# Spreading 1/rms over a tile: two products with ones and diagonals in place of eight narrow products

## The chip, the cores and the metric

The kernel runs on one core of a Trainium2 chip. A core has a matrix engine (TensorE, "PE" in the profile, its weight loads "PEld"), two elementwise engines that can read the matrix engine's accumulator PSUM (VectorE, "DVE", and ScalarE, "ACT"), a third one for data in SBUF alone (GpSimd, "POOL"), and SyncE ("SP"), which issues transfers. Each engine works through its own queue in order, and semaphores make one wait for another. The metric is the time of one execution on the device in microseconds; shown is the median of several runs.

## The reference

One decoder layer on x of 2048 rows by 1024 columns, float32:

```
hn   = rmsnorm(x, norm1_g)
proj = hn @ w_in                      # u_pool (512) | q | k | v (512 each)
mixed = concat(rmsnorm(pool_mixer(u_pool)), rmsnorm(stick_breaking(q, k, v)))
h = x + mixed @ w_out
h = h + square(relu(rmsnorm(h) @ w_up)) @ w_down
y = rmsnorm(h)
# rmsnorm(x, g) = x * rsqrt(mean(x*x, over columns) + 1e-6) * g
```

What matters here is rmsnorm: each row of the sequence has one factor 1/rms, and every value of that row is multiplied by it.

## The kernel before

Activations are held transposed: a tile has 128 features in its partitions and 512 rows of the sequence along its free dimension, so the 2048 rows make four row blocks (`j` = 0 to 3) of eight feature chunks each. In this layout the factor 1/rms differs along the free dimension and is the same in all 128 partitions. To multiply by it with an elementwise engine, the 512 factors have to stand in every partition; bringing them there is the "spread".

Every matrix product is done in three passes of a split of both operands into a high and a low part (`split`, L143 and L144: ACT copies to the reduced type, DVE subtracts), which gives the three lines L172 to L174 of `products`.

A normalisation goes through these steps:

- `add_square` (L177): ACT squares a chunk into a buffer tagged `nt` (pool `ntp`, three buffers), and DVE adds it to the tile `ss`.
- `mean_squares` (L194): tiny products (eight instructions) with a column 1/n sum `ss` over the partitions, 128 rows of the sequence at a time, into four columns of PSUM (`pm`, L199).
- `inv_root` (L203): DVE takes the four columns out of PSUM (L207), and then POOL (in one early case DVE) computes the inverse root on a tile of 128x4: one integer operation and three Newton steps.
- in `inv_rms`, `yr` (L235, L236) becomes the high and the low part of these 128x4 factors: factor number 128*b + p stands in partition p, column b.
- `spread` (L221): for each of the four columns b and for high and low part, one product whose stationary operand is the column repeated 128 times and whose moving operand is the identity `identr`; eight products of 128 columns each write a tile `pr` of 128x512 in PSUM.
- ACT copies `pr` to SBUF as `r` (L245), and `normed` (L251) multiplies each chunk by its gain and by `r` (L257, tile `nt`) and splits the result into `h` or `mix`. For the first row block the products are made with x before it is normalised, and `r` is applied when they leave PSUM (L373, L418, L430).

`inv_rms` is used in the front of the kernel: for the first norm of the four row blocks, for the pooled part and for the attention part of each, and for the second norm of row blocks 0 and 1. The second norm of blocks 2 and 3 (`root_last`, with spreads inside `up`) and the final norm (`final_root`, `final_put`) call `spread` directly.

The front runs input projections, the pool mixer and the attention together: `prog` is a list of projection steps, `run` (L1256) emits them one after the other, and between them takes pieces of normalisation from the list `later` and pieces of attention from `todo`. A scheduling pass then orders each engine's queue by priority and by the times that it expects instructions to be ready. The body of `inv_rms` has high priority. `gates` makes TensorE's steps after a certain count stand behind the sums (`pm`) and behind the spread (`pr`). After the front, from about 700 us on, come the two large products `up` (L983) and `down` (L1218). A second version of the whole attention stands in a branch at the end that these inputs don't take.

Of the kernel before, what the change touches and what calls it, by code (L numbers as in the profile page):

```python
# [8 lines left out]
F32 = mybir.dt.float32  # L9
F32R = mybir.dt.float32r  # L10
BF16 = mybir.dt.bfloat16
I32 = mybir.dt.int32
AF = mybir.ActivationFunctionType
ALU = mybir.AluOpType

P = 128
# [11 lines left out]
TB = T // P  # L28
# [18 lines left out]
def hymba_block(ctx: ExitStack, tc: tile.TileContext, xT, gains, w_in, pool_w, w_out, w_up, w_down, out):  # L47
    nc = tc.nc
# [3 lines left out]
    const = pool("const", 1)  # L52
# [43 lines left out]
    ident = const.tile([P, P], F32, name="ident")  # L96
    make_identity(nc, ident)
    identr = const.tile([P, P], F32R, name="identr")
    nc.vector.tensor_copy(identr, ident)
    identb = const.tile([P, P], BF16, name="identb")  # L100
    nc.vector.tensor_copy(identb, ident)
    maskb = const.tile([P, 2, P], BF16, name="maskb")
# [44 lines left out]
    marks, gates = {}, []  # L147
# [46 lines left out]
    def mean_squares(parts, n, where=None, tag="px"):  # L194

        pm = (where or psx).tile([P, T], F32, tag=tag, name="pm")
        for c in range(TB):
            for i, ss in enumerate(parts):
                marks["pm"] = nc.tensor.matmul(pm[:, c:c + 1], ss[:, c * P:(c + 1) * P], inv[n],  # L199
                                               start=(i == 0), stop=(i == len(parts) - 1))  # L200
        return pm[:, 0:TB]

    def inv_root(pm, eng):  # L203

        v, w = vp.tile([P, 3 * TB], F32, tag="v", name="v"), pm.shape[-1]
        m, y, t = v[:, 0:w], v[:, TB:TB + w], v[:, 2 * TB:2 * TB + w]
        nc.vector.tensor_scalar(m, pm, 1.0, EPS, op0=ALU.mult, op1=ALU.add)  # L207
        eng.tensor_scalar(y.bitcast(I32), m.bitcast(I32), -0.5, float(0x5F3759DF), op0=ALU.mult, op1=ALU.add)
        for _ in range(3):
            if eng is nc.vector:  # L210
                eng.scalar_tensor_tensor(t, y, -0.5, y, op0=ALU.mult, op1=ALU.mult)
                eng.tensor_tensor(t, t, m, ALU.mult)
                eng.scalar_tensor_tensor(y, t, 1.5, y, op0=ALU.add, op1=ALU.mult)
            else:
                eng.tensor_tensor(t, y, y, ALU.mult)
                eng.tensor_tensor(t, t, m, ALU.mult)
                eng.tensor_scalar(t, t, -0.5, 1.5, op0=ALU.mult, op1=ALU.add)
                eng.tensor_tensor(y, y, t, ALU.mult)
        return y

    def spread(pr, yr):  # L221

        for b in range(TB):
            for x in range(2):
                mm = nc.tensor.matmul(pr[:, b * P:(b + 1) * P], yr[:, x, b:b + 1].to_broadcast([P, P]), identr,  # L225
                                      start=(b == 0 and x == 0), stop=(b == TB - 1 and x == 1), skip_group_check=True)
        return mm

    def inv_rms(ss, n, r=None, eng=None, early=False):

        eng = eng or nc.gpsimd
        with tc.high_priority():
            y = inv_root(mean_squares([ss], n, psz if early else None, "pz" if early else "px"), eng)
            yr = tmp.tile([P, 2, TB], F32R, tag="yr", name="yr")
            eng.tensor_copy(yr[:, 0], y)  # L235
            eng.tensor_tensor(yr[:, 1], y, yr[:, 0].bitcast(F32), ALU.subtract)  # L236
            where, tag = (psx, "px") if eng is nc.vector else (psz, "pz") if early else (pst, "pt")
            pr = where.tile([P, T], F32, tag=tag, name="pr")
            marks["pr"] = spread(pr, yr)
            if eng is not nc.vector:  # L240
                g = state["tick"]
                gates.extend([(g + 10, marks["pm"]), (g + 14, marks["pr"])])
            if r is None:
                r = tmp.tile([P, T], F32, tag="r", name="r", bufs=2)
            nc.scalar.activation(r, pr, AF.Copy)  # L245
            return r

    def rms(chunks):
        return inv_rms(sum_squares(chunks), len(chunks) * P)
# [79 lines left out]
    def norm1_first():  # L329

        x, h = st[0]["x"], []
        for k in range(KD):
            d = make_h(0)
            a = nc.scalar.activation(d[:, 0], x[:, k], AF.Copy, scale=g1[:, k:k + 1])
            v = nc.vector.scalar_tensor_tensor(d[:, 1], x[:, k], g1[:, k:k + 1], d[:, 0].bitcast(F32),
                                               op0=ALU.mult, op1=ALU.subtract)
            h.append((d[:, 0], d[:, 1]))
        st[0]["h"] = h
        with tc.issue_after(a.ins), tc.issue_after(v.ins):
            ss = sum_squares([x[:, k] for k in range(KD)])  # L340
        st[0]["r"] = inv_rms(ss, D, root_tile(), nc.vector)

    def norm1_rms(j):
        def square(k):
            if k == 0:
                st[j]["ss"] = sum_tile()
            add_square(st[j]["ss"], st[j]["x"][:, k], k == 0)
        later.extend(lambda k=k: square(k) for k in range(KD))
        later.append(lambda: st[j].update(r=inv_rms(st[j]["ss"], D, root_tile() if j == 2 else None, early=j == 1)))
# [1046 lines left out]
```

## Time and profile before

| | |
|---|---|
| runs shown | 1949.64 us median of 3, 1944.7 to 1951.38 |
| profiled execution | 1947.63 us, its span 1945.8 us |
| granted TensorE clock, mean | 0.997 |
| busy PE / DVE / ACT / POOL | 1922.0 / 1267.6 / 954.2 / 201.2 us |

A row of the timeline reads: start and length in microseconds, engine, line, operation, written tile <- read tiles, shapes, count, and in square brackets how long the engine stood idle before it and for what. A row of the groups gives, after the bar, the busy time of the whole group in us and the mean length of one in ns, and after the next bar the idle time before them. A matmul's length in the timeline (0.39 us for 512 columns) is longer than the distance to the next one, since they are pipelined; the chain of work gives the distance.

### The profile page before, as it was taken

How to read it: one execution, taken by the hardware profiler on the slowest of the kernel's cores; microseconds unless marked ns; L12 is line 12 of the kernel's file. 1: busy time of each engine (PE TensorE's matmuls, PEld its weight loads, DVE VectorE, ACT ScalarE, POOL GpSimd, SP SyncE). 2: the span in 40 equal slices, each digit the busy share in tenths (PEclk: the TensorE clock that was granted, in tenths of full speed). 3: DMA queues.
4: the chain of work that ended last, by engine and by line, in shares of the span. 5: the costliest groups of instructions: out<-in, count | busy, mean ns of one | idle time of the engine just before them, and what ended most of it. 6: DMA issues, size and time to landing. Idle time of an engine off the chain costs nothing.

```text
span 1945.8 us, 26005 instructions
## 1 busy us (share of the span) xinstructions
PE 1922.0 (99%) x9139; PEld 1602.9 (82%) x9139; DVE 1267.6 (65%) x1882; ACT 954.2 (49%) x1544; POOL 201.2 (10%) x399
## 2 busy tenths in 40 slices
PE   9999999999999999999999999999999999999997
PEld 7888888888888888888878888878888888888887
DVE  6887799668866975777586565655554443446474
ACT  5565566455644555555575555553323232424353
POOL 0212113113211110000000000000110000213010
PEclk9999999999999999999999999999999999999999
DMA  6686686898796854677474534478876554646472
GB/s 216 205 263 200 205 287 200 259 323 281 247 386 219 322 200 149 217 242 252 171 244 155 173 141 163 148 253 292 299 273 196 194 195 152 199 156 205 150 253 89
DMA packets 164845, 426.79 MB, mean 219 GB/s; under 512 B 19680, under 2 KB 25824, under 8 KB 160608
## 3 DMA queue, kind: packets, MB, share of 16 engines
q1 hardware_dynamic: 164560, 424.77, 64.3%
q8 instruction: 74, 1.21, 0.3%
q14 instruction: 67, 0.55, 0.1%
q10 hardware_dynamic: 144, 0.26, 0.0%
HBM read 284.44 MB, written 140.51 MB: 218 GB/s over the span
## 4 chain that ended last, share of the span: by engine, by line
PE 93%; DVE 2%; DMA 2%; ACT 1%; issue 1%; POOL 1%; SPq 0%; ACTq 0%; DVEq 0%; POOLq 0%
PE pb L1218 31%; PE pY L983 17%; PE pZ L983 8%; PE pd L172 8%; PE pd L174 8%; PE pd L173 8%; PE pX L983 4%; PE po L676 2%; PE pta L669 1%; PE pr L225 1%; PE pz L611 1%; PE pz L612 1%; PE pm L199 1%; DMA wr<-in_w_down_dram 1%; PE pb L1181 1%
## 5 line engine op out<-in xcount | busy, mean ns | idle before, releaser
L1218 PE MATMUL pb<-ad,wd 128*128 128x512 f32 x2640 | 601.5, 390 | 1.6 <-ACT ad L143 1.0
L1218 PEld LDWEIGHTS pb<-ad,wd 128*128 128x128 f32 x2640 | 494.9, 188 | 104.8 <-ACT ad L143 1.6
L983 PE MATMUL pY<-sa,hw 128*128 128x512 f32 x1536 | 364.3, 389 | 2.2 <-ACT u L922 2.2
L983 PEld LDWEIGHTS pY<-sa,hw 128*128 128x128 f32 x1536 | 288.1, 188 | 62.7 <-ACT u L922 3.0
L172 PE MATMUL pd<-h,hl 128*128 128x512 f32 x752 | 299.0, 398 | 0.7 <-DVE qkr L418 0.7
L173 PE MATMUL pd<-h,hl 128*128 128x512 f32 x752 | 297.3, 395 | 0.0
L174 PE MATMUL pd<-h,hl 128*128 128x512 f32 x752 | 296.3, 394 | 0.9 <-DVE hl L144 0.9
L983 PE MATMUL pZ<-sa,hw 128*128 128x512 f32 x768 | 184.7, 389 | 1.4 <-DVE a L936 1.4
L143 ACT ACTIVATE ad<-ar 128x1024 fp32r<-128x1024 f32 x112 | 117.3, 1050 | 138.0 <-PE pb L1218 126.2
L144 DVE TENSOR_TENSOR wd<-wr,wd 128x1024 fp32r<-128x1024 f32 x64 | 82.8, 1294 | 151.0 <-ACT wd L143 150.8
L144 DVE TENSOR_TENSOR ad<-ar,ad 128x1024 fp32r<-128x1024 f32 x112 | 144.1, 1292 | 55.9 <-ACT ad L143 55.8
L143 ACT ACTIVATE wd<-wr 128x1024 fp32r<-128x1024 f32 x64 | 67.8, 1059 | 209.1 <-PE pb L1218 204.9
L983 PEld LDWEIGHTS pZ<-sa,hw 128*128 128x128 f32 x768 | 144.0, 188 | 31.6 <-DVE a L936 1.9
L174 PEld LDWEIGHTS pd<-h,hl 128*128 128x128 f32 x752 | 141.5, 188 | 29.2 <-DVE hl L144 1.4
L172 PEld LDWEIGHTS pd<-h,hl 128*128 128x128 f32 x752 | 141.8, 189 | 28.4 <-DVE qkr L418 1.0
L173 PEld LDWEIGHTS pd<-h,hl 128*128 128x128 f32 x752 | 141.5, 188 | 26.2
L143 ACT ACTIVATE hl<-raw 128x512 fp32r<-128x512 f32 x168 | 103.8, 630 | 106.5 <-PE pd L174 64.5
L144 DVE TENSOR_TENSOR hl<-raw,hl 128x512 fp32r<-128x512 f32 x168 | 114.0, 685 | 46.4 <-ACT hl L143 45.7
L144 DVE TENSOR_TENSOR hw<-rt,hw 128x512 fp32r<-128x512 f32 x128 | 87.5, 686 | 75.3 <-ACT hw L143 75.2
L983 PE MATMUL pX<-sa,hw 128*128 128x512 f32 x384 | 93.1, 389 | 0.0
L1013 DVE TENSOR_TENSOR wr<-wr 128x1024 f32<-128x1024 f32 x32 | 39.2, 1224 | 81.3 <-DMA wr<-in_w_down_dram 78.3
L922 ACT ACTIVATE u<-pY 128x512 f32<-128x512 f32 x64 | 38.1, 595 | 102.6 <-PE pY L983 102.4
(203 smaller groups left out, 2391.0 us busy)
## 6 DMA issues: line engine op xcount, KB each, us to landing
ar<-sd SPq DMA_DIRECT2D x112, 512.0 KB, 4.5
wr<-in_w_down_dram SPq DMA_DIRECT2D x72, 512.0 KB, 3.7
rb<-in_w_up_dram SPq DMA_DIRECT2D x32, 1024.0 KB, 5.9
sd<-a SPq DMA_DIRECT2D x128, 256.0 KB, 3.8
raw<-in_w_in_dram SPq DMA_DIRECT2D x50, 512.0 KB, 4.5
sd<-s SPq DMA_DIRECT2D x96, 256.0 KB, 3.7
raw<-in_w_out_dram SPq DMA_DIRECT2D x32, 512.0 KB, 4.9
sr<-su SPq DMA_DIRECT2D x28, 512.0 KB, 5.5
```

The lines of the kernel that those rows point to most:

```text
L143: nc.scalar.activation(hi, src, AF.Copy)
L144: return nc.vector.tensor_tensor(lo, src, hi.bitcast(F32), ALU.subtract)
L172: nc.tensor.matmul(ps, hl[:, 0, c], hi, start=(k == 0), stop=False)
L173: nc.tensor.matmul(ps, hl[:, 0, c], lo, start=False, stop=False)
L174: mm = nc.tensor.matmul(ps, hl[:, 1, c], hi, start=False, stop=(k == n - 1))
L199: marks["pm"] = nc.tensor.matmul(pm[:, c:c + 1], ss[:, c * P:(c + 1) * P], inv[n], start=(i == 0), stop=(i == len(parts) - 1))
L225: mm = nc.tensor.matmul(pr[:, b * P:(b + 1) * P], yr[:, x, b:b + 1].to_broadcast([P, P]), identr, start=(b == 0 and x == 0), stop=(b == TB ...
L676: nc.tensor.matmul(po[:, p * 256 + to:p * 256 + to + hi - lo], vw[:, 2 * p + v], at[:, x, lo:hi], start=(p == 0 and n == 0 and x == 0), sk ...
L922: nc.scalar.activation(k[name], y, AF.Copy)
L983: nc.tensor.matmul(t, w[:, wx, c], a[:, ax, c % 2], start=first and c == 0 and x == 0, stop=last and c == G - 1 and x == 2, skip_group_che ...
L1013: nc.vector.tensor_tensor(b, a, b, ALU.subtract)
L1218: nc.tensor.matmul(ps[q, n], t[:, wx, c, n * P:(n + 1) * P], left_[q][:, ax, c], start=(n_ in ("P1", "P5", "P2") and kk == 0 and c == 0 an ...
```

## The change

In `inv_rms` alone the call of `spread` is replaced. Two tiles of 128x4x128 (`diag`, taken from the `nt` buffers) get, in block b, the identity times column b of `yr`: DVE makes the one for the high part in a single product of two repeated operands, ACT the one for the low part in four copies of the identity with a scale per partition. Then two products of 512 columns, with a stationary 128x128 tile of ones (`onesr`, made once at the start by DVE), sum each diagonal tile over the partitions into `pr`. The direct calls of `spread` stay.

```
+    onesr = const.tile([P, P], F32R, name="onesr")
+    nc.vector.tensor_scalar(onesr, ident, 0.0, 1.0, op0=ALU.mult, op1=ALU.add)
...
             pr = where.tile([P, T], F32, tag=tag, name="pr")
-            marks["pr"] = spread(pr, yr)
+
+            whole = [P, TB, P]
+            diag = [ntp.tile(whole, F32R, tag="nt", name="diag") for _ in range(2)]
+            nc.vector.tensor_tensor(diag[0], ident.rearrange("p (o c) -> p o c", o=1).to_broadcast(whole),
+                                    yr[:, 0].bitcast(F32).rearrange("p (b o) -> p b o", o=1).to_broadcast(whole), ALU.mult)
+            for b in range(TB):
+                nc.scalar.activation(diag[1][:, b], ident, AF.Copy, scale=yr[:, 1, b:b + 1].bitcast(F32))
+            for x in range(2):
+                marks["pr"] = nc.tensor.matmul(pr, onesr, diag[x].rearrange("p b c -> p (b c)"), start=(x == 0), stop=(x == 1))
```

## The prediction

> **What bounds the kernel now.** I read the summary of engines first, then the busy time by stretches, the waits of TensorE from 50 to 700 us (where the front's work lies), and the chain of work that ended last around one spread.
>
> ```profile
> span 1945.8 us, 26005 instructions
> PE 1922.0 (99%) x9139; PEld 1602.9 (82%) x9139; DVE 1267.6 (65%) x1882; ACT 954.2 (49%) x1544; POOL 201.2 (10%) x399
> ```
>
> TensorE is busy for 99% of the span. The other engines have room on average, but the average hides stretches:
>
> ```profile
> 40.00:80.00 40.00, 39.53 (x186) 32.50 (x184) 37.50 (x67) 20.54 (x35) 8.30 (x22) 1.00 0.64 199
> ...
> 300.00:400.00 100.00, 100.00 (x559) 85.72 (x558) 79.12 (x133) 56.03 (x104) 24.56 (x50) 1.00 0.72 235
> ```
>
> The columns are stretch, its length, busy time of PE, PE's weight loads, DVE, ACT and POOL, then the granted clock (1.00). From 40 to 80 us DVE works 37.5 of 40 us; around 300 it works 79%, ACT 56%. TensorE's waits in the front are short:
>
> ```profile
> PE pr L225 <- POOL yr L235: 1.2, 1, 1.2
> PE pd L174 <- DVE hl L144: 0.9, 1, 0.9
> PE pd L172 <- DVE qkr L418: 0.7, 1, 0.7
> ```
>
> These are the three longest; one of them is a spread waiting for POOL. No entry names the normalised chunks (`nt`, then `h`) that follow r, so a slightly later r is not what TensorE waits for today. So a microsecond taken off TensorE's queue in the front should come off the time, and one added to what its queue waits for should go on.
>
> **The change, part by part.** *Count.* Each call of `inv_rms` ends with one copy of the spread values on ACT, so those copies count the calls that ran:
>
> ```profile
> L245 ACT ACTIVATE r<-pr x12: 587/597/600, 39.1 to 626.9; 128x512 f32<-128x512 f32 x12
> L245 ACT ACTIVATE ra<-pr x2: 597/598/600, 566.4 to 618.4; 128x512 f32<-128x512 f32 x2
> ```
>
> That is 14. The other spreads (two for the last tiles, three at the end) call `spread` directly and stay as they are.
>
> *Removed and added on TensorE.* A spread in the chain:
>
> ```profile
> 185.93 0.23 PE pd L173
> ...
> 188.42 0.23 PE pd L172
> 188.65 0.84 PE pr L225 x8
> 189.49 0.35 PE pta L669 x3
> ```
>
> Columns: start, length, what. Eleven 512-wide products take 188.42 - 185.93 = 2.49 us, 0.226 each. The eight 128-wide products of the spread take 0.84, 0.105 each, nearly half of a product four times as wide. Two 512-wide products in their place take 2 x 0.226 = 0.45. The saving is 0.39 per spread, 14 x 0.39 = 5.5 us, all on the engine that bounds.
>
> [...]
>
> *Added on ACT and DVE.* No row shows the new operations; these are the nearest:
>
> ```profile
> L334 ACT ACTIVATE h<-xt,gains 128x512 fp32r<-128x512 f32 x8 | 5.4, 714 | 2.5 <-DMA xt<-in_xT_dram 2.5
> ...
> L1195 ACT ACTIVATE fsh<-p,gains 128x256 f32<-128x256 f32 x6 | 3.0, 494 | 0.0
> ...
> 12.14 2.58 ACT L334 ACTIVATE h<-xt,gains 128x512 fp32r<-128x512 f32 x4
> ...
> L183 DVE TENSOR_TENSOR ss<-ss,sq 128x512 f32<-128x512 f32 x73 | 49.9, 684 | 6.5 <-ACT sq L182 5.5
> ...
> 39.76 1.29 DVE L418 TENSOR_TENSOR qkr<-pd,r 128x512 f32<-128x512 f32 x2 [2.38 <-ACT r L245]
> ```
>
> ACT copies with a scale per partition: 714 ns at 512 columns, 494 at 256, so 0.86 ns a column and an estimated 384 ns at 128. Four of 512 in a row take 2.58, so each after the first adds 0.62, 0.09 under its own length; four of 128 take 0.38 + 3 x 0.29 = 1.26 us. DVE's product of two 128x512 operands takes 0.68, and two in a row 1.29, so it holds DVE for 0.60. Bounds: for ACT from 4 x 0.25 = 1.0 (half of the 256-column one each) to 4 x 0.49 = 2.0 (no cheaper than it); for DVE 0.60 in a full queue to 0.68 alone. I take 1.26, the straight line through the two sizes. DVE and ACT work side by side, so ACT's 1.26 and two hand-overs of about 0.05 set it: the matmuls can start about 1.4 us after POOL has written yr, where they start at once today.
>
> ACT's 14 x 1.26 = 18 us and DVE's 14 x 0.60 = 8 us lie beside TensorE's work wherever the engine is not the last; that cover is the 44% of ACT and 21% of DVE left idle in the stretch at 300.
>
> *Does TensorE wait for the diagonals?* POOL's last write of yr and the first product of the spread, at the six narrowest sites and, last, the next one:
>
> ```profile
> 69.86 0.20 POOL L236 TENSOR_TENSOR yr<-v,yr 128x4 fp32r<-128x4 f32 x1
> 70.62 0.22 PE L225 MATMUL pr<-identr,yr 128*128 128x128 f32 x1
> ...
> 187.40 0.20 POOL L236 TENSOR_TENSOR yr<-v,yr 128x4 fp32r<-128x4 f32 x1
> 188.49 1.00 PE L225 MATMUL pr<-identr,yr 128*128 128x128 f32 x8
> ...
> 390.31 0.20 POOL L236 TENSOR_TENSOR yr<-v,yr 128x4 fp32r<-128x4 f32 x1
> 391.14 1.06 PE L225 MATMUL pr<-identr,yr 128*128 128x128 f32 x8
> 392.24 0.60 ACT L245 ACTIVATE r<-pr 128x512 f32<-128x512 f32 x1 [5.06 <-PE pr L225]
> ...
> 461.38 0.33 PE L225 MATMUL pr<-identr,yr 128*128 128x128 f32 x1 [1.24 <-POOL yr L235]
> 461.41 0.20 POOL L236 TENSOR_TENSOR yr<-v,yr 128x4 fp32r<-128x4 f32 x1
> ...
> 563.75 0.20 POOL L236 TENSOR_TENSOR yr<-v,yr 128x4 fp32r<-128x4 f32 x1
> 565.12 0.22 PE L225 MATMUL pr<-identr,yr 128*128 128x128 f32 x1
> ...
> 616.06 0.20 POOL L236 TENSOR_TENSOR yr<-v,yr 128x4 fp32r<-128x4 f32 x1
> 617.15 0.22 PE L225 MATMUL pr<-identr,yr 128*128 128x128 f32 x1
> ...
> 525.98 0.71 POOL L236 TENSOR_TENSOR yr<-v,yr 128x4 fp32r<-128x4 f32 x1
> 529.05 0.22 PE L225 MATMUL pr<-identr,yr 128*128 128x128 f32 x1
> ```
>
> From the end of the write to the product there are 0.56, 0.89, 0.63, none, 1.17 and 0.89 us, then 2.36. If the spread kept its place in TensorE's queue, the waits would grow by 0.84, 0.51, 0.77, 1.63 (from 461.38 to 461.61 + 1.4), 0.23 and 0.51: 4.5 us. At the other eight sites the room is 2.36 or wider, and they are left at nothing. With ACT at its upper bound, 0.74 longer, the six would add another 4.4. If the planner puts the spread later by as much as the diagonals take, with other products ahead of it, the addition is nothing; and the 1.24 could go. Between 0 and 4.5 I take 1.5: thirteen of the fourteen were placed late enough for a chain of fifteen POOL instructions, so the planner's times are mostly cautious, and the row nearest to a miss is the single 1.24.
>
> *The dense stretch of DVE.* The stretch from 40 to 80 us, with DVE at 37.5 of 40, ends in a wait of TensorE; the spread at 70 lies inside it:
>
> ```profile
> 56.05 0.69 DVE L144 TENSOR_TENSOR hl<-raw,hl 128x512 fp32r<-128x512 f32 x1 [1.11 <-ACT hl L143]
> ...
> 80.24 0.50 PE L172 MATMUL pd<-h,hl 128*128 128x512 f32 x1 [0.70 <-DVE qkr L418]
> ```
>
> One more DVE product there pushes qkr back by its 0.60, and TensorE's 0.70 with it: +0.6. The first spread's r also comes later (by up to 1.4, if nothing moves), but the 1.11 us in which DVE stands idle for weights takes that up.
>
> *Edits at nothing.* The `ones` tile is one 128x128 operation on DVE before the first data: DVE then waits 2.92 us.
>
> ```profile
> 5.18 0.69 DVE L144 TENSOR_TENSOR hl<-raw,hl 128x512 fp32r<-128x512 f32 x1 [2.92 <-ACT hl L143]
> ```
>
> The two diagonals take two of the three `nt` buffers; the squares before them are summed by then, and the first `nt` after them needs r, so it comes behind the matmuls that free both. Without that cover a chunk would wait for one 512-wide product, 0.23. No DMA is added or moved; SP's and POOL's queues keep their order. Behind the new instructions stand, on ACT, weight splits and the copy of r, on DVE, their second halves and PSUM evacuations; ACT already stands still 5.06 us for r at 392 without a TensorE wait.
>
> *Sum.* -5.5 + 0.6 + 1.5 = -3.4 us. The profiled execution took 1947.63 (span 1945.8 and 1.8 around it), so 1944.2 in its terms; the median shown is 2.0 higher, 1949.64, and so the forecast is 1946.2.
>
> **The rivals.**
> *Placed later everywhere.* The planner sets each spread behind its diagonals, no wait is added, and the 1.24 at 461 goes: -5.5 - 1.2 = -6.7, 1942.9. For it: thirteen spreads met their yr in time. Against: the dense DVE stretch.
>
> *DVE becomes the bound in the front (the slower side).* The diagonal has high priority, so it stands early in DVE's queue, and DVE, in order, waits there for POOL while evacuations stand behind it. DVE has one such wait today, for the sums:
>
> ```profile
> DVE v L207 <- PE pm L199: 2.5, 3, 1.5
> ```
>
> That is 0.83 each. A diagonal then costs 0.60 + 0.83 = 1.43 of DVE, and at the 79% of sites where DVE is busy, 11 of 14, TensorE loses it: 15.7 - 5.5 = +10.2, 1959.8. It decides from (5.5 + 5.85) / 1.43, 8 sites, on. Against it: the present waits of TensorE for DVE are few.
>
> *TensorE saves nothing.* If the array were charged by columns alone, eight times 128 are as many as twice 512: 0 + 0.6 + 1.5 = +2.1, 1951.7. [...] Against it stands 0.84 against 0.45.
>
> **How the numbers follow.** 0.3% is 5.85 us, about what a measurement of this kernel can tell from no change. Chances: forecast 0.45 (its own range from -5.5 to -5.5 + 0.6 + 4.5 + 4.4 = +4.0, 1944.1 to 1953.6), later everywhere 0.22, DVE 0.25, no saving 0.08. Faster is the second, 0.22; slower is DVE with a tail of the last, 0.27; the rest, 0.51, within. The range from 1940 reaches 3 us under the faster case and up to 1960 takes in about half of DVE's, which leaves out some 0.17.
>
> **What would show it.** The spread's line should show 28 products of 128x512 in the front at the length of their neighbours; PE's busy time should fall by about 5 us before 700 us and not after. A wait of TensorE at the spread for the ACT diagonals would confirm the 1.5, and one of 1.3 at 80 us the 0.6. Wrong it would be if DVE's wait for yr appears in front of the diagonal at many sites, or if the planner orders the attention pieces otherwise, so that new waits of TensorE appear at lines that the change does not touch.

## The result and the profile after

The changed kernel takes 1958.37 us (median of 6 runs, 1955.39 to 1959.16) against 1948.94 for the kernel before (6 runs, 1943.18 to 1951.38). The ratio is 1.0051, with a 95% interval of 1.004 to 1.0062: 9 to 10 us slower. Forecast was 3.4 us faster; the range, up to 1960, holds the time, but the sign is wrong. The profiled execution took 1955.39 us, its span 1953.5.

The page of the changed kernel, its span and engines:

```profile
span 1953.5 us, 25880 instructions
PE 1922.0 (98%) x9055; PEld 1598.7 (82%) x9055; DVE 1279.1 (65%) x1897; ACT 970.7 (50%) x1600; POOL 200.1 (10%) x399
```

TensorE has 84 matmuls less (14 x 6) and is busy for the same 1922.0 us. Its mean granted clock is 0.994 in place of 0.997, and 0.3% of 1922 us is 5.8 us, an estimate of what the slower products add; the fewer products should take off 5.5. In the chain of work the new spread stands at 125 us as follows (start, length, what):

```profile
125.15 0.23 PE pd L176
125.39 0.48 PE pr L249 x2
125.87 1.09 PE po L686 x10
```

Two products take 0.48 in place of 0.84, so the saving of the spread itself is there. What came in its place is waits of TensorE at other lines. Its waits from 50 to 705 us (line that waits, line waited for: total, times, longest), some of them:

```profile
PE po L686 <- ACT sg L629: 1.8, 1, 1.8
PE pd L174 <- DVE qkr L428: 1.4, 1, 1.4
PE pd L174 <- ACT h L145: 1.2, 1, 1.2
PE pd L174 <- ACT sq L184: 1.1, 1, 1.1
PE pd L174 <- DVE acc L785: 1.1, 1, 1.1
...
PE pr L249 <- DVE diag L244: 0.2, 1, 0.2
```

Only the last, 0.2 us, is a wait at the spread. The others are attention, projections and output projection that wait for ACT or DVE. Before, the longest three were 1.2, 0.9 and 0.7, and the first of those was the spread's own. All rows of this view come to 12.6 us, against 4.3 us before (50 to 700 us). The groups of the new instructions, and after the second bar the idle time of their engine before them:

```profile
L247 ACT ACTIVATE diag<-ident,yr 128x128 fp32r<-128x128 f32 x56 | 17.9, 391 | 42.1 <-POOL yr L238 42.1
L249 PE MATMUL pr<-diag,onesr 128*128 128x512 f32 x28 | 10.5, 415 | 0.2 <-DVE diag L244 0.2
L244 DVE TENSOR_TENSOR diag<-ident,yr 128x512 fp32r<-128x512 f32 x14 | 9.7, 691 | 15.3 <-POOL yr L237 15.3
```

The work was sized rightly (ACT 17.9, DVE 9.7). But ACT stood still for 42.1 us in front of the diagonals and DVE for 15.3, both waiting for POOL, with their other work queued behind. Part of that wait is made by the change itself. POOL's last operation, for which ACT waits, takes 0.70 us in the median where it took 0.20 (median is the middle figure; before, then changed):

```profile
L236 POOL TENSOR_TENSOR yr<-v,yr x13: 198/199/709, 69.9 to 622.7; 128x4 fp32r<-128x4 f32 x13
```

```profile
L238 POOL TENSOR_TENSOR yr<-v,yr x13: 200/702/706, 68.9 to 641.0; 128x4 fp32r<-128x4 f32 x13
```

DVE's product for the diagonal runs at the same time (at one site 568.79 to 569.48, POOL's operation 568.84 to 569.55). Thirteen times 0.50 is 6.5 us, an estimate of its part in the 42.1. And the order of the squares changed. ACT in the changed kernel, from the attention norm of block 2 (`sq<-ol`) to the second norm of block 0 (`sq<-acc`):

```profile
556.58 1.14 ACT L184 ACTIVATE sq<-ol 128x512 f32<-128x512 f32 x2
569.58 1.28 ACT L247 ACTIVATE diag<-ident,yr 128x128 fp32r<-128x128 f32 x4 [3.25 <-POOL yr L238]
570.76 0.62 ACT L184 ACTIVATE sq<-acc 128x512 f32<-128x512 f32 x1
...
588.60 1.28 ACT L247 ACTIVATE diag<-ident,yr 128x128 fp32r<-128x128 f32 x4 [10.30 <-POOL yr L238]
592.04 0.60 ACT L255 ACTIVATE r<-pr 128x512 f32<-128x512 f32 x1
```

and the same in the kernel before:

```profile
550.79 1.14 ACT L182 ACTIVATE sq<-ol 128x512 f32<-128x512 f32 x2
551.84 0.62 ACT L182 ACTIVATE sq<-acc 128x512 f32<-128x512 f32 x1
...
573.42 0.60 ACT L245 ACTIVATE r<-pr 128x512 f32<-128x512 f32 x1 [0.83 <-PE pr L225]
```

Before, the squares of the second norm followed at once and its r came at 573; now they come behind the diagonals of the first, and its r at 592. How much of the loss comes from this late r is not shown; with buffers of its own (below) r comes at 580, and the front is no shorter. The end of the front moves, and TensorE has less to do right behind it: the busy time from 700 to 720 in the changed kernel, and in the kernel before for the 20 us around the same point (the first products of `up`, 701.7 and 695.4):

```profile
700.00:720.00 20.00, 17.62 (x75) 14.24 (x74) 17.16 (x22) 14.46 (x20) 4.25 (x5) 0.91 0.85 295
```

```profile
694.00:714.00 20.00, 20.00 (x97) 16.81 (x96) 15.14 (x20) 13.21 (x19) 5.69 (x13) 1.00 0.57 200
```

75 products in place of 97, at a mean clock of 0.91. The chain of work leads back from TensorE's wait there, through ACT, to a transfer of the weights of `up`, which starts behind a piece of DVE's work (a split `sa`, done at 701.5):

```profile
701.94 7.97 DMA rb<-in_w_up_dram
...
712.66 4.53 PE pY L993 x12
```

Since the execution's start and the products after the front differ a little from one to the next, a table below also gives a length of the front in the profiled execution: from the first sums (the first start of `v<-pm`) to the first product of `up` (the first start of `pY`). The rows for the kernel before, and then for the changed one:

```profile
L207 DVE TENSOR_SCALAR v<-pm x19: 135/154/164, 30.9 to 1900.1; 128x4 f32<-128x4 f32 x19
L983 PE MATMUL pY<-sa,hw x1536: 387/389/502, 695.4 to 1307.2; 128*128 128x512 f32 x192
```

```profile
L209 DVE TENSOR_SCALAR v<-pm x19: 140/161/164, 30.3 to 1907.5; 128x4 f32<-128x4 f32 x19
L993 PE MATMUL pY<-sa,hw x1536: 387/389/797, 701.7 to 1316.6; 128*128 128x512 f32 x192
```

So 695.4 - 30.9 = 664.5 us before and 701.7 - 30.3 = 671.4 after, 6.9 longer; the 22 products missing at the start of `up` are another 22 x 0.226 = 5.0 us.

### The profile page after: what moved, and what is told of

Read it like the earlier page. It is cut to its first block, busy times and chain, and to the rows that moved or that the text cites. A ratio compares the mean times of both kernels' runs of the same rounds, so it can differ in the third digit from the quotient of the medians.

```text
span 1953.5 us, 25880 instructions
## 1 busy us (share of the span) xinstructions
PE 1922.0 (98%) x9055; PEld 1598.7 (82%) x9055; DVE 1279.1 (65%) x1897; ACT 970.7 (50%) x1600; POOL 200.1 (10%) x399
## 4 chain that ended last, share of the span: by engine, by line
PE 82%; DVE 7%; DMA 6%; issue 1%; ACT 1%; POOL 1%; SPq 1%; DVEq 0%; ACTq 0%; POOLq 0%
PE pb L1228 31%; PE pY L993 17%; PE pZ L993 8%; PE pd L174 5%; PE pd L176 5%; PE pd L175 5%; PE pX L993 4%; DMA raw<-in_w_in_dram 1%; PE po L686 1%; DMA xt<-in_xT_dram 1%; DVE hl L146 1%; PE pta L679 1%; DVE pc L633 1%; PE pb L1191 1%; DVE s L391 1%
```

## The experiments

Each time is compared with runs of the kernel before on the same chip, as a ratio with its 95% interval.

### TensorE's part alone

```
             pr = where.tile([P, T], F32, tag=tag, name="pr")
-            marks["pr"] = spread(pr, yr)
+            wide = identr.rearrange("p (o c) -> p o c", o=1).to_broadcast([P, TB, P])
+            for x in range(2):
+                marks["pr"] = nc.tensor.matmul(pr.rearrange("p (b c) -> p b c", b=TB),
+                    yr[:, x, 0:1].to_broadcast([P, P]), wide, start=(x == 0), stop=(x == 1))
```

> Two 512-wide products per spread and nothing new on DVE or ACT: the low and high part of the first column of yr are multiplied with the identity repeated four times, so all four blocks get the factors of the first block (this part of the computation is changed). Load theory (the loss of the change comes from 14 x 0.6 us on DVE and 14 x 1.3 us on ACT): this kernel shows the saving alone, 5 to 5.5 us under before, about 1943.5. Order theory (the loss comes from waits of TensorE at other lines because the planner orders the queues anew whenever the spread's times move): TensorE's slots at the spread fall by 5 us, but other waits differ from before by several us in either direction, so the time may lie anywhere from 1938 to 1958, with new waits at lines that the edit does not touch.

Measured: 1939.73 us, ratio 0.9962 (0.9948 to 0.9976), 7.4 us faster. Its front:

```profile
L207 DVE TENSOR_SCALAR v<-pm x19: 134/155/164, 28.8 to 1891.2; 128x4 f32<-128x4 f32 x19
L985 PE MATMUL pY<-sa,hw x1536: 387/389/500, 687.9 to 1299.8; 128*128 128x512 f32 x192
```

659.1 us, 5.4 shorter than before: the forecast 5.5 of the saving. The saving is real, and the new order of the queues that comes with it brings no loss of its own; the loss of the change lies in what it adds beside TensorE: work and waits on ACT and DVE, held buffers, a later r.

### The side work, with the narrow products kept

```
+            one = tmp.tile([P, TB], F32, tag="one", name="one")
+            eng.tensor_scalar(one, yr[:, 1].bitcast(F32), 0.0, 1.0, op0=ALU.mult, op1=ALU.add)
+            whole = [P, TB, P]
+            diag = [ntp.tile(whole, F32R, tag="nt", name="diag") for _ in range(2)]
+            nc.vector.tensor_tensor(diag[0], <ident repeated>, <one repeated>, ALU.mult)
+            for b in range(TB):
+                nc.scalar.activation(diag[1][:, b], ident, AF.Copy, scale=one[:, b:b + 1])
-            marks["pr"] = spread(pr, yr)
+            marks["pr"] = spread(pr, yr, diag)      # diag[x][:, b] in place of identr
```

> The eight narrow products are kept, and the diagonal work is added in front of them: one DVE product 128x512 and four ACT copies 128x128 with a scale that is exactly one (made on POOL from yr, one small operation more), whose results the eight products read in place of the identity. Load theory: the loss of the change without its saving, 9.4 + 5 = 14 us over before, about 1963, with TensorE waiting for DVE and ACT results. Latency theory (r comes 1.4 to 2 us later): the same sign, waits at the lines that read r or h. Order theory: somewhere between 1945 and 1965, with the waits at other places than in the changed kernel.

Measured: 1968.47 us, ratio 1.011 (1.0093 to 1.0127), 21 us slower. That is more than the 14 expected, and it needs no new products on TensorE. This run has the work, the waits, the held buffers and a later r together, and one small operation more on POOL, so it doesn't say which of them costs.

### A later r, nothing else

```
+            if eng is not nc.vector:
+                for _ in range(4):          # and 10 in a second kernel
+                    eng.tensor_scalar(y, y, 1.0, 0.0, op0=ALU.mult, op1=ALU.add)
             eng.tensor_copy(yr[:, 0], y)
```

> The kernel before with four more multiplications by one (128x4) on POOL in each inverse root, so yr and r come 1 to 2 us later; nothing is added to TensorE, DVE or ACT and POOL is 10% busy. Load theory: no change, within 2 us of before. Latency theory: slower by part of the 9.4 us. Order theory: the queues come out in another order, and the time moves by several us in either direction although no busy engine has more to do.

> The kernel before with ten more multiplications by one (128x4) on POOL in each inverse root: r comes about 3 us later, as late as with the diagonals on POOL, with no work for other engines and no nt buffer held. If a late r were the cause of the 13 us there, this kernel would be 8 to 13 us slower than before; by the buffer theory it is within 4 us of before, like the 2 us that four such operations cost.

Measured: with four, 1949.46 us, ratio 1.0012 (1.0002 to 1.0021); with ten, 1959.2 us, ratio 1.0051 (1.0034 to 1.0068). At one site (near 390 us) the four take from 387.42 to 388.50, 1.1 us, and the ten from 392.34 to 395.41, 3.1 us. So a delay of 1.1 us costs about 2 us when taken alone, and one of 3.1 costs 10, the first of the two cases expected for ten; the 4 us that the buffer theory allowed are exceeded. The change's own delay lies between the two: ACT's four copies take 1.28 us, and POOL's last operation 0.50 more than before, an estimated 1.8 us in all. What a late r alone costs the change is so known only to lie between some 2 and 10 us.

### The diagonals on POOL

```
-            nc.vector.tensor_tensor(diag[0], ...)
-            for b in range(TB):
-                nc.scalar.activation(diag[1][:, b], ident, AF.Copy, scale=yr[:, 1, b:b + 1].bitcast(F32))
+            for x in range(2):
+                nc.gpsimd.tensor_tensor(diag[x], <ident repeated>, <yr[:, x] repeated>, ALU.mult)
```

> The changed kernel with both diagonal tiles made by POOL (two products 128x512, about 1.6 us each) in place of DVE and ACT. Load theory: the saving remains and the loss goes, about 1943.5. Latency theory: r is about 2 us later than in the changed kernel, so slower than it, over 1958. Order theory: 1940 to 1960, new waits of TensorE at lines not touched.

Measured: 1960.43 us, ratio 1.0075 (1.0054 to 1.0096). DVE and ACT have nothing to do for the spread here and wait for nothing of it, and it is as slow as the change. The two products take 1.04 us each on POOL, so r is later by two and the nt buffers are held longer. This run does not tell those two apart: a delay of 3.1 us alone costs 10 (above), and held buffers alone cost 10 too (next).

### The buffers, from both sides

Buffers of their own for the diagonals:

```
-            diag = [ntp.tile(whole, F32R, tag="nt", name="diag") for _ in range(2)]
+            dp = olp if state["pieces"] == 3 else pa
+            diag = [dp.tile(whole, F32R, tag="dg", name="diag", bufs=2) for _ in range(2)]
```

> The changed kernel with the two diagonal tiles in two buffers of their own instead of two of the three nt buffers that the squares and normalised chunks use; everything else is as in the change, its ACT and DVE instructions too. Buffer theory (the diagonals sit in the ring of nt buffers while POOL computes, so the squares of the next norm, which need one, can't start): most of the loss goes, about 1943 to 1947, the squares after a diagonal no longer come behind it, and the second norm of block 0 gets its sums near 560 us again instead of 583. Queue theory (ACT and DVE, in order, stand at the diagonal until POOL has written yr, 42 and 15 us in the changed kernel): no change from it, about 1957.

and two nt buffers held in the kernel before:

```
-            yr = tmp.tile([P, 2, TB], F32R, tag="yr", name="yr")
-            eng.tensor_copy(yr[:, 0], y)
-            eng.tensor_tensor(yr[:, 1], y, yr[:, 0].bitcast(F32), ALU.subtract)
+            yr = [ntp.tile([P, T], F32R, tag="nt", name="yr")[:, 0:TB] for _ in range(2)]
+            eng.tensor_copy(yr[0], y)
+            eng.tensor_tensor(yr[1], y, yr[0].bitcast(F32), ALU.subtract)
```

> The kernel before, eight narrow products and no diagonals, with the high and the low part of yr (128x4 each) written by POOL into two of the nt buffers instead of a small tile of their own. No engine has more work and nothing new waits on ACT or DVE. Buffer theory: 8 to 15 us slower than before, about 1955 to 1962, with the squares of the next norm behind the spread. Queue theory: no change, 1946 to 1950.

Measured: own buffers 1954.92 us, ratio 1.0035 (1.0025 to 1.0046); held in the kernel before 1959.03 us, ratio 1.005 (1.0033 to 1.0066). Holding the buffers alone costs 10 us, with not one microsecond of work added to any engine. Giving the change its own buffers wins back 3 us, though the two intervals (1.0025 to 1.0046, and 1.004 to 1.0062 for the change) overlap. The squares move back to where they were (own buffers, ACT, the first of the second norm):

```profile
555.89 1.14 ACT L184 ACTIVATE sq<-ol 128x512 f32<-128x512 f32 x2
556.93 0.62 ACT L184 ACTIVATE sq<-acc 128x512 f32<-128x512 f32 x1
...
580.06 0.60 ACT L256 ACTIVATE r<-pr 128x512 f32<-128x512 f32 x1 [1.79 <-PE pr L250]
```

In the kernel that holds them, the squares of the second norm of block 0 start at 564.04 (551.84 before) and then wait for one another, through DVE's sum. The front is 701.5 - 31.2 = 670.3 us, 5.8 longer than before. The rest of the loss stands at the start of `up`. There TensorE, in order, waits for the root of block 3 and works at a lower clock (0.84 from 700 to 730 us); one operation of 128x4 on POOL in that root takes 5.22 us, where its line has a median of 0.195:

```profile
568.96 0.63 ACT L182 ACTIVATE sq<-acc 128x512 f32<-128x512 f32 x1 [0.76 <-DVE ss L183]
...
715.93 5.22 POOL L217 TENSOR_SCALAR v<-v 128x4 f32<-128x4 f32 x1
...
PE pr L225 <- POOL yrlast L782: 5.7, 1, 5.7
...
700.00:730.00 30.00, 23.88 (x104) 19.43 (x103) 17.61 (x24) 13.71 (x21) 8.97 (x15) 0.84 0.54 194
```

DVE works without a gap from 712.13 to 721.10, and POOL's operation ends at 721.15. The run with the side work and the narrow products has the same at this place, 5.23 us. So the held buffers set off the loss, but in this execution (1962.0 us, the slowest of its runs) 5.7 us of it come through this operation, and why it takes so long was not tested.

So the buffers are one cause, but the change with its own is still 7 us slower than before and 15 slower than TensorE's part alone.

### Both diagonals on DVE, own buffers

```
-            nc.vector.tensor_tensor(diag[0], ...)
-            for b in range(TB):
-                nc.scalar.activation(diag[1][:, b], ident, AF.Copy, scale=yr[:, 1, b:b + 1].bitcast(F32))
+            for x in range(2):
+                nc.vector.tensor_tensor(diag[x], <ident repeated>, <yr[:, x] repeated>, ALU.mult)
```

> Buffers of their own, and both diagonal tiles by DVE (two products, 1.2 us), none by ACT. Buffer theory: as with own buffers, about 1943 to 1947. Queue theory: the 42 us of ACT's waits go and DVE's grow from 15 to about 20; half or more of the loss goes, 1945 to 1952.

Measured: 1950.77 us, ratio 1.0012 (1.0002 to 1.0022). Without ACT's part another 4 us go, within what the queue theory gave: ACT's waits and its work at the diagonals weigh more than 11 us more work on DVE (busy 1284.5 us against 1273.5).

### Work and wait, one at a time and together

All four have TensorE's part as above and own buffers or none. Work alone:

```
+            nc.vector.tensor_tensor(diag[0], <ident repeated>, <a constant repeated>, ALU.mult)
+            for b in range(TB):
+                nc.scalar.activation(diag[1][:, b], ident, AF.Copy, scale=inv[D])
```

> Two wide products as in the run with TensorE's part alone (column 0 for all four blocks, so that part of the computation is changed), and beside them the same DVE product 128x512 and four ACT copies 128x128 per spread as in the change, made from constants in buffers of their own, which nobody reads: the work without the wait for POOL and without a later r. Work theory (the 8 us on DVE and 18 us on ACT are what costs): 8 to 12 us over the run with TensorE's part alone, 1948 to 1952. Wait theory (the engines stand in order behind POOL): within 3 us of it, 1939 to 1943.

Wait alone:

```
+            yc = tmp.tile([P, 2, TB], F32R, tag="yc", name="yc")
+            nc.vector.tensor_copy(yc[:, 0], yr[:, 0].bitcast(F32))
+            nc.scalar.activation(yc[:, 1], yr[:, 1].bitcast(F32), AF.Copy)
             # the two wide products read yc in place of yr
```

> Two wide products of column 0 again (that part of the computation is changed), whose stationary operand is copied from yr by one DVE and one ACT instruction of 128x4: DVE and ACT wait for POOL at the same place as in the change, with hardly any work, r about 0.5 us later, no nt buffer held. Wait theory: ACT stands some 35 us and DVE some 15 us at these copies, and the time is 8 to 12 us over the run with TensorE's part alone, 1948 to 1952. Work theory: within 3 us of it, 1939 to 1943.

Both, with the diagonals made from yr and read by nobody:

> As the run with the wait alone, and the diagonals besides, made by DVE and ACT from yr in buffers of their own; TensorE reads only the small copies (column 0, that part of the computation is changed) and not the diagonals. Work, wait and saving are then those of the change with its own buffers, but r comes about 1.2 us sooner. If the parts add up, the front ends 9 us later than with TensorE's part alone, near 697 us, and the time is 1947 to 1951. If work and wait make each other worse, it is as slow as the change with its own buffers: front near 704, time 1953 to 1956.

And the wait with a later r (the high part goes through four more copies on POOL before TensorE reads it):

> As the run with the wait alone, and the high part of yr goes through four more copies of 128x4 on POOL before TensorE reads it (column 0, that part of the computation is changed): DVE and ACT wait as there, r comes about 1.2 us later, no work is added to them. If a late r and the wait make each other worse, the front ends near 699 and the time is 1950 to 1954; if a late r alone costs what it costs without the wait (2 us), the time is 1946 to 1949.

| | time, us | ratio to before | front, us | against TensorE's part alone |
|---|---|---|---|---|
| TensorE's part alone | 1939.73 | 0.9962 (0.9948 to 0.9976) | 659.1 | |
| + work | 1944.18 | 0.9977 (0.9965 to 0.9989) | 662.3 | +3.2 in the front |
| + wait | 1946.8 | 0.9992 (0.998 to 1.0003) | 663.4 | +4.3 |
| + wait, r later | 1947.42 | 0.9993 (0.9981 to 1.0005) | 663.4 | +4.3 |
| + work and wait | 1949.34 | 1.001 (1.0 to 1.002) | 669.2 | +10.1 |
| + TensorE reads the diagonals (own buffers) | 1954.92 | 1.0035 (1.0025 to 1.0046) | 674.7 | +15.6 |
| the change (nt buffers) | 1958.37 | 1.0051 (1.004 to 1.0062) | 671.4, and 5.0 at the start of `up` | +12.3 and 5.0 |

The front is read from one profiled execution, the time from all of them. The profiled execution of the run with work and wait took 1952.62 us, 3.3 more than its median, and that of the run with a later r 1945.35, 2.1 less; so the sums below go by the time.

In the run with the wait alone, ACT's and DVE's waits come to nearly those of the change (54 us against 57), on instructions of 128x4:

```profile
ACT yc L241 <- POOL yr L236: 33.2, 13, 4.8
...
DVE yc L240 <- POOL yr L235: 20.9, 11, 3.2
```

That is 54 us of two engines standing still, and it costs the time some 6 us (0.9992 - 0.9962 of 1948), while 27.6 us of work cost 3. The wait is clear of the noise; the work is not, since its interval overlaps that of TensorE's part alone. The two engines don't stand still longer in all than before, either: from 20 to 700 us ACT is busy for 377.4 us and DVE for 544.6 with the wait alone, for 373.2 and 541.7 in the kernel before. So idle time as such is not the price; that the work behind the copies comes later is the likely one, and was not followed site by site. Neither theory as I put it, one cause and 8 to 12 us from it, held: work gave 3 and wait 6. Together they cost 9 by the time, their sum, as expected if the parts add up. A later r by four operations adds nothing measurable to the wait, so the case in which these two make each other worse is not borne out. TensorE's reading the diagonals adds another 5 us (1.0035 - 1.001). What in it costs this was not separated: r comes behind the work, the wait and the hand-over, and POOL's last operation takes 0.70 us again (0.20 in the run with work and wait, where a short copy stands first on DVE). Nor was it looked into which of the consumers of r pays for it.

### The same saving without the side work

```
-            yr = tmp.tile([P, 2, TB], F32R, tag="yr", name="yr")
-            eng.tensor_copy(yr[:, 0], y)
-            eng.tensor_tensor(yr[:, 1], y, yr[:, 0].bitcast(F32), ALU.subtract)
...
-            marks["pr"] = spread(pr, yr)
+            for b in range(TB):
+                marks["pr"] = nc.tensor.transpose(pr[:, b * P:(b + 1) * P], y[:, b:b + 1].to_broadcast([P, P]), ident)
```

> The kernel before with the eight narrow products of each spread in the front replaced by four transposes of the repeated column of y in float32, without the split into high and low part: TensorE's transposes take 0.11 to 0.12 us each in the chain before, so 0.45 in place of 0.84 per spread, POOL has two operations less, and nothing is added to DVE or ACT. If the saving on TensorE is real and the loss of the change comes from what DVE, ACT and the buffers have to do, about 5 us under before: 1940 to 1944.

In a second kernel the direct spreads of the last blocks and of the final norm are replaced in the same way:

> The same transposes in all nineteen spreads, those of the two last row blocks and of the final norm too: another 5 x 0.4 = 2 us, 1938 to 1943, if these stand on TensorE's path as the others do.

Measured: in the front alone 1941.36 us, ratio 0.9964 (0.9954 to 0.9974); in all spreads 1935.38 us, ratio 0.9934 (0.9915 to 0.9952). A transpose of a column repeated 128 times is a spread: four instructions, in float32, from y itself. In the chain:

```profile
185.96 0.44 PE pr L237 x4
```

0.44 where eight products took 0.84, with no work for DVE and ACT, two operations less on POOL and no buffer. Both are faster than either kernel. The second takes 1935.38 us where 1938 to 1943 were expected, some 13 under the kernel before; the two intervals do not overlap, and why five more spreads are worth more than 2 us was not looked into.

## Why the prediction was wrong

- *The saving on TensorE (-5.5).* Right. The front is 5.4 us shorter with TensorE's part alone, and the rival in which TensorE saves nothing is refuted here: 0.84 for the eight narrow products against 0.48 for the two wide ones.
- *Work beside TensorE's, at nothing.* Wrong, mis-sized. The 27.6 us of work were sized about rightly (17.9 and 9.7 against 18 and 8), but the cover of 44% idle ACT and 21% idle DVE is not shown to be free: they cost some 3 us alone, at the edge of the noise.
- *What stands behind the new instructions.* This step failed most. I named the queues behind the diagonals and put their price at nothing, because ACT had stood still 5.06 us for r without harm. I had that wait as the rival, on DVE and at 0.83 us a site; in fact DVE waits 15.3 / 11 = 1.4 and ACT 42.1 / 13 = 3.2 us a time, and ACT, which I left out of the rival, is the larger. A high priority places the instruction early in the queue, and then POOL is late; some 6.5 us of ACT's wait come from POOL's own last operation becoming slower, which I had not thought of. The wait costs some 6 us alone.
- *The spread waits for its diagonals (+1.5).* Wrong in its place. TensorE waits 0.2 us there in all, because the planner did put the spreads later (the end that I gave as nothing); near 570 us, for one, at 570.86 ACT's copies are done, and the first product follows at 572.98. But reading the diagonals costs about 5 us further on, and the premise that a slightly later r is not what TensorE waits for holds for small delays alone: 1.1 us cost 2, 3.1 us cost 10.
- *The dense stretch of DVE at 80 us (+0.6).* Right in kind, too small. TensorE now waits three times there, 0.32 + 1.16 + 1.37 = 2.85 us against 0.70 before:

```profile
75.29 0.50 PE L401 MATMUL pp<-pls,pw 128*128 128x512 f32 x1 [0.32 <-ACT yb L404]
77.42 0.50 PE L174 MATMUL pd<-h,hl 128*128 128x512 f32 x1 [1.16 <-ACT h L145]
79.29 0.50 PE L174 MATMUL pd<-h,hl 128*128 128x512 f32 x1 [1.37 <-DVE qkr L428]
```

- *Two nt buffers at nothing.* Wrong. I looked at the squares ahead of the diagonals and at the chunks that follow r, but not at the squares of the next norm, which may start while POOL computes and need a buffer of the same ring. Holding two of three costs 10 us in the kernel before (5.7 of it, in the profiled execution, through the slow operation on POOL), and some 3 in the change; the intervals of the change with and without its own buffers overlap, so the 3 is less sure than the 10.
- *The `ones` tile at nothing.* Nothing in the profile speaks against it.

Of the rivals, the one on the slower side had the right mechanism, a wait in order for POOL at the head of a queue, and its +10.2 is near the measured +9.4. That is partly chance: it charged DVE alone, took DVE's busy share for the share of sites, and the runs split the loss over work, wait, the reading of the diagonals and buffers.

## What to carry to other kernels

In this kernel, with the bound engine 99% busy, what was put on the engines with idle time was not free: their work and wait together cost 9 us. So look at what will stand behind the new instruction in that engine's queue while it waits for its input, and at how many sites. The length of the wait is not its price: 54 us of waiting cost some 6 here. Before a tile is put in a shared ring of buffers, follow all users of the ring, those that could run during the wait too, and not only those before and after. And look for a form in which the bound engine alone does less: four transposes gave the whole saving (ratio 0.9964, against 0.9962 for TensorE's part alone), with nothing moved to anybody else.

## What was not expected of the hardware

TensorE's clock falls in the middle of the kernel, though TensorE stands still there for no longer than 1.75 us at a time. In the changed kernel, from 205 to 227 us (the clock is the figure behind POOL's busy time):

```profile
205.00:211.00 6.00, 6.00 (x32) 5.00 (x31) 6.00 (x12) 3.50 (x7) 0.00 (x0) 1.00 0.25 90
211.00:217.00 6.00, 2.74 (x12) 1.78 (x10) 6.00 (x12) 4.20 (x8) 2.67 (x1) 0.76 0.76 239
217.00:221.00 4.00, 3.91 (x9) 3.14 (x10) 4.00 (x9) 1.72 (x3) 0.21 (x2) 0.50 0.86 249
221.00:227.00 6.00, 6.00 (x30) 4.92 (x29) 2.55 (x6) 2.53 (x5) 0.00 (x0) 1.00 0.50 142
```

Finer stretches put the fall between 214.0 and 214.5 and the return at 221.0; all those between show 0.50:

```profile
213.50:214.00 0.50, 0.30 (x1) 0.19 (x1) 0.50 (x2) 0.00 (x0) 0.00 (x0) 1.00 1.18 229
214.00:214.50 0.50, 0.06 (x1) 0.00 (x0) 0.50 (x2) 0.27 (x1) 0.17 (x1) 0.67 0.67 238
...
220.50:221.00 0.50, 0.50 (x2) 0.40 (x2) 0.50 (x2) 0.00 (x0) 0.00 (x0) 0.51 0.85 201
```

The longest waits from 211 to 217:

```profile
213.70 0.36 PE L686 MATMUL po<-at,vw 128*128 128x256 f32 x1 [1.75 <-ACT sg L629]
214.72 0.90 PE L686 MATMUL po<-at,vw 128*128 128x256 f32 x3 [0.67 <-DVE at L146]
...
217.09 0.79 PE L402 MATMUL pp<-pls,pw 128*128 128x512 f32 x1 [0.93 <-DVE pls L146]
```

TensorE was busy for 2.74 of 6 us, and from 217 to 221, almost without a wait (busy for 3.91 of 4 us), it ran at half its clock (0.50): a 512-wide product every 0.43 us (218.11, 218.53, 218.96 in the timeline) in place of 0.23. Nine products at 0.2 us more are 1.8 us on top of the waits, an estimate from these rows. In the kernel before the same place has waits of 0.22, 0.43 and 0.58, TensorE is busy for 4.85 of the 6 us from 211 to 217, and the clock is 1.00. The clock fell after one wait of 1.75 us (until 213.70) and a single product, between 214.0 and 214.5, before the second wait was over at 214.72. When it returned, at 221.0, TensorE had been at work since 217.09, for 3.9 us. So here the waits of TensorE may have cost more than their own length, by the estimated 1.8 us; what decides when the clock falls and returns is not shown by this one place.
